# An encoder step in fp32: two accumulators per weight tile, products with high weight parts first

## The chip, the cores and the metric

The kernel runs on one core of a Trainium2 chip. The metric is the device time of one launch in microseconds (us), lower is better; times given are medians over runs of the same program. All inputs and outputs are fp32 and lie in device memory at the start and at the end.

## The reference

One step of a streaming encoder with two layers over 640 token rows (512 of a new prompt, 8 running streams of 16), width 1024. Layer 0 is a convolution module and a gated feed-forward block, then one shared key and value are projected, layer 1 is attention over chunks and a second feed-forward block. What the change touches is layer 0:

```python
def swiglu_ffn(h, g, w_in, w_out):                 # w_in 1024 x 5632, w_out 2816 x 1024
    a, b = jnp.split(rms_norm(h, g) @ w_in, 2, axis=-1)
    return h + (jax.nn.silu(a) * b) @ w_out

def conv_module(h, hist, g, w_pw1, b_pw1, w_dw, b_dw, ln_g, ln_b, w_pw2, b_pw2):
    a, gate = jnp.split(rms_norm(h, g) @ w_pw1 + b_pw1, 2, axis=-1)
    glu = a * jax.nn.sigmoid(gate)
    full = jnp.concatenate([hist.astype(glu.dtype), glu], axis=1)
    y = lax.conv_general_dilated(                  # depthwise, 31 taps, causal
        full, w_dw[:, None, :].astype(full.dtype), window_strides=(1,), padding="VALID",
        dimension_numbers=("NWC", "WIO", "NWC"), feature_group_count=D_MODEL) + b_dw
    y = jax.nn.silu(layer_norm(y, ln_g, ln_b))
    return h + y @ w_pw2 + b_pw2, full[:, -CONV_HIST:]
...
    # run_trunk: layer 0 = conv_module, swiglu_ffn; layer 1 = attention, swiglu_ffn; final rms_norm
```

## The kernel before, in words

Activations are kept transposed, features on the 128 partitions and tokens along the free axis, in two groups: group 0 has 256 columns, group 1 has 384. So a weight tile is the stationary operand of a matmul, and the tokens stream past.

An fp32 product is made of three matmuls in a rounded type. `wsplit` loads a tile of 128 x 2048 weights into `raw` (SP's queue, L139), copies it to the high part `whi` on ScalarE (L150) and takes the low part `wlo` = raw − whi in two pieces (L154): part of the columns on VectorE, and `pool` quarters of them on POOL (three quarters in the feed-forward block of layer 0, two in the second projection). Each of the three tiles has two buffers, so a load must wait until the subtraction of the tile two before it has read `raw`. Activations are split alike (`xsplit`, L159 on ScalarE, L160 on VectorE). `mm3` then runs, for each of the 8 slices along the contraction, the products high·high (L170), low weight·high (L171) and high weight·low (L172) into one accumulator in PSUM. There are four such accumulators (`mmt`, tile name `mm`).

A weight tile of the first projection, and of the feed-forward block's input, feeds two accumulators (`ab`: the value and the gate). `glu` and `ffn_in` fill the first with `mm3`, then the second. `pw2` (second projection of the convolution module) and `ffn_out` also have two outputs per weight tile, one after the other.

The depthwise convolution is shared out by channel block: on VectorE (`conv`, L434 and L437, one operation per tap), on ScalarE and POOL (`conv_pool`, L416 and L417), and on TensorE (`conv_pe`, L469). For the last, `conv_pe_load` stores a block of `gs` or `gp` (the GLU's outputs) to a scratch `sc` in device memory (L452) and reads it back four times with a shift into `x4` (L455, shown as `x<-sc` in the profile); these transfers stand in SP's queue like the weight loads. LayerNorm (`conv_ln`) takes means by summing blocks on POOL (L195) and then over partitions on TensorE (L204); L226 and L230 make the power −1/2, L216 spreads it over the partitions, and L489 multiplies by it.

The string `PLAN` lists the steps of layer 0 (a and b: `glu` of the two groups, l and p: loading and running the convolution on TensorE, q and d: the convolution on POOL and VectorE, n: LayerNorm, w: `pw2`, r: the norm before the feed-forward block, f: one chunk of that block for group 0). This is the order in which the program is written. The final order on each engine is then made by a scheduler ahead of time, from its own estimates and from priorities: what is written under `tc.high_priority` is put forward. So an edit of one helper can move instructions on all engines. On the chip each engine takes its own list strictly in order. A chunk of the feed-forward block is 6 tiles of `ffn_in`, then 4 weight tiles of `ffn_out` whose results VectorE adds to the residual `h` (L303). After the three chunks written in `PLAN` come a shared one and three of group 1.

Attention and the second feed-forward block (L968, L913) use code of their own.

## Time and profile before

| | |
|---|---|
| median of 3 runs | 1549.51 us (1548.63 to 1552.37) |
| profiled execution, its own time | 1551.3 us |
| span of the profile | 1549.5 us |
| mean granted clock of TensorE | 0.984 |
| TensorE matmuls | 10770 recorded, busy 1471.7 us (95%) |
| VectorE busy | 1050.1 us (68%) |
| ScalarE busy | 662.4 us (43%) |
| POOL busy | 443.8 us (29%) |
| moved by DMA | 199.95 MB, mean 129 GB/s |

The span is the time between the first and the last instruction that the profiler saw on the core. "PE" is TensorE's matmul stream and "PEld" its weight loads, which run beside matmuls; DVE is VectorE, ACT ScalarE, POOL GpSimd, and SPq the queue in which SP issues transfers. L numbers are lines of the kernel before. In rows of the timeline the bracket names the idle time ahead of the instruction and what ended it.

### The profile page before, as it was taken

How to read it: one execution, taken by the hardware profiler on the slowest of the kernel's cores; microseconds unless marked ns; L12 is line 12 of the kernel's file. 1: busy time of each engine (PE TensorE's matmuls, PEld its weight loads, DVE VectorE, ACT ScalarE, POOL GpSimd, SP SyncE). 2: the span in 40 equal slices, each digit the busy share in tenths (PEclk: the TensorE clock that was granted, in tenths of full speed). 3: DMA queues.
4: the chain of work that ended last, by engine and by line, in shares of the span. 5: the costliest groups of instructions: out<-in, count | busy, mean ns of one | idle time of the engine just before them, and what ended most of it. 6: DMA issues, size and time to landing. Idle time of an engine off the chain costs nothing.

```text
span 1549.5 us, 26569 instructions
## 1 busy us (share of the span) xinstructions
PE 1471.7 (95%) x10770; PEld 1398.9 (90%) x10770; DVE 1050.1 (68%) x1863; ACT 662.4 (43%) x1173; POOL 443.8 (29%) x403
## 2 busy tenths in 40 slices
PE   5888998989999999999999999999989999999997
PEld 5878888989999999999988798886989999999997
DVE  6994999988555455457576767566796476476455
ACT  4544454535423323235454445443554244244244
POOL 6865568877501000001321211110411121121110
PEclk9999999999999999999999999998999999999998
DMA  7784434444421333433655545453103213213211
GB/s 236 234 228 142 137 113 159 148 157 153 147 82 55 129 116 129 135 118 126 202 183 201 174 140 205 133 175 114 55 28 109 82 56 109 82 55 109 82 55 68
DMA packets 59658, 199.95 MB, mean 129 GB/s; under 512 B 10128, under 2 KB 22672, under 8 KB 46736
## 3 DMA queue, kind: packets, MB, share of 16 engines
q1 hardware_dynamic: 59248, 197.96, 39.1%
q8 instruction: 84, 1.38, 0.4%
q10 hardware_dynamic: 288, 0.31, 0.1%
q14 instruction: 38, 0.31, 0.1%
HBM read 187.02 MB, written 11.22 MB: 128 GB/s over the span
## 4 chain that ended last, share of the span: by engine, by line
PE 71%; DVE 16%; ACT 3%; issue 3%; DMA 3%; POOL 2%; SPq 0%; POOLq 0%; DVEq 0%; ACTq 0%
PE mm L170 12%; PE mm L172 12%; PE mm L171 12%; PE pb L968 6%; DVE w L437 5%; DVE wlo L154 4%; PE pc L968 4%; PE pa L968 4%; PE pb L170 1%; PE pb L171 1%; PE pb L172 1%; PE pa L172 1%; PE pa L170 1%; PE pc L170 1%; PE pc L172 1%
## 5 line engine op out<-in xcount | busy, mean ns | idle before, releaser
L171 PE MATMUL mm<-x,wlo 128*128 128x256 f32 (+1 forms) x1344 | 416.8, 312 | 15.4 <-DVE wlo L154 14.9
L170 PE MATMUL mm<-x,whi 128*128 128x256 f32 (+1 forms) x1344 | 413.3, 312 | 6.4 <-ACT x L159 3.7
L172 PE MATMUL mm<-x,whi 128*128 128x256 f32 (+1 forms) x1344 | 412.7, 311 | 0.5
L150 ACT ACTIVATE whi<-raw 128x2048 fp32r<-128x2048 f32 (+2 forms) x117 | 197.7, 1694 | 232.6 <-PE mm L172 138.8
L171 PEld LDWEIGHTS mm<-x,wlo 128*128 128x128 f32 x1344 | 257.1, 192 | 18.7 <-DVE wlo L154 17.5
L170 PEld LDWEIGHTS mm<-x,whi 128*128 128x128 f32 x1344 | 254.5, 191 | 11.2 <-ACT x L159 4.1
L172 PEld LDWEIGHTS mm<-x,whi 128*128 128x128 f32 x1344 | 255.1, 191 | 2.9 <-DVE x L160 1.8
L154 DVE TENSOR_TENSOR wlo<-raw,whi 128x2048 fp32r<-128x2048 f32 (+5 forms) x117 | 214.0, 1832 | 62.2 <-ACT whi L150 61.2
L154 POOL TENSOR_TENSOR wlo<-raw,whi 128x1536 fp32r<-128x1536 f32 (+3 forms) x50 | 145.7, 2918 | 69.0 <-ACT whi L150 69.0
L913 POOL TENSOR_TENSOR raw<-raw 128x512 f32<-128x512 f32 x38 | 50.5, 1330 | 332.3 <-DVE raw L913 257.5
L171 PE MATMUL mm<-hid,wlo 128*128 128x256 f32 (+1 forms) x352 | 107.7, 308 | 6.6 <-DVE wlo L154 6.6
L172 PE MATMUL mm<-hid,whi 128*128 128x256 f32 (+1 forms) x352 | 105.8, 307 | 0.2
L170 PE MATMUL mm<-hid,whi 128*128 128x256 f32 (+1 forms) x352 | 104.6, 307 | 0.1
L437 DVE SCALAR_TENSOR_TENSOR w<-gp,dwv,w 128x384 f32<-128x384 f32 x180 | 103.9, 612 | 0.8
L195 POOL TENSOR_TENSOR acc<-sq,sq 128x384 f32<-128x384 f32 (+1 forms) x8 | 8.1, 1006 | 258.2 <-ACT sq L179 258.1
L171 PEld LDWEIGHTS mm<-hid,wlo 128*128 128x128 f32 x352 | 66.0, 188 | 7.8 <-DVE wlo L154 7.8
L417 POOL TENSOR_TENSOR y<-y,cvt 128x256 f32<-128x256 f32 (+1 forms) x60 | 69.3, 1154 | 6.3 <-ACT cvt L416 4.0
L172 PEld LDWEIGHTS mm<-hid,whi 128*128 128x128 f32 x352 | 65.7, 188 | 0.6 <-DVE hid L160 0.6
L159 ACT ACTIVATE whi<-raw 128x1024 fp32r<-128x1024 f32 x38 | 39.4, 1054 | 61.6 <-PE pc L172 18.1
L170 PEld LDWEIGHTS mm<-hid,whi 128*128 128x128 f32 x352 | 65.2, 188 | 0.4 <-ACT hid L159 0.3
L968 PE MATMUL pa<-x0f,whi 128*128 128x320 f32 x228 | 61.2, 316 | 2.5 <-DVE t L913 2.3
L195 POOL TENSOR_TENSOR acc<-acc,sq 128x384 f32<-128x384 f32 (+1 forms) x48 | 52.7, 1097 | 28.9 <-ACT sq L179 27.5
(317 smaller groups left out, 3391.4 us busy)
## 6 DMA issues: line engine op xcount, KB each, us to landing
raw<-in_w_in SPq DMA_DIRECT2D x62, 1024.0 KB
raw<-in_w_out SPq DMA_DIRECT2D x36, 768.0 KB
raw<-in_w_pw SPq DMA_DIRECT2D x22, 1024.0 KB
cache<-in_ck SPq DMA_DIRECT2D x32, 512.0 KB
cache<-in_cv SPq DMA_DIRECT2D x32, 512.0 KB
raw<-in_w_kq SPq DMA_DIRECT2D x8, 1024.0 KB
x<-sc SPq DMA_DIRECT2D x16, 368.0 KB
raw<-in_w_out SPq DMA_DIRECT2D x4, 1024.0 KB
```

What stands on the lines that cost most here:

```text
L150: nc.scalar.activation(out=hi[:, a:b], in_=raw[:, a:b], func=AF.Copy)
L154: eng.tensor_tensor(out=lo[:, a:b], in0=raw[:, a:b], in1=hi[:, a:b].bitcast(F32), op=ALU.subtract)
L159: nc.scalar.activation(out=hi, in_=src, func=AF.Copy)
L170: nc.tensor.matmul(ps, wh, xh, start=(i == 0), stop=False)
L171: nc.tensor.matmul(ps, wl, xh, start=False, stop=False)
L172: nc.tensor.matmul(ps, wh, xl, start=False, stop=(i == last))
L195: last["acc"] = eng.tensor_tensor(out=acc[:, :n], in0=prev, in1=s(), op=ALU.add)
L417: nc.gpsimd.tensor_tensor(out=y[g][:, c, :], in0=y[g][:, c, :], in1=pr[:, :n], op=ALU.add)
L437: nc.vector.scalar_tensor_tensor(out=dst, in0=src, scalar=wj, in1=dst, op0=ALU.mult, op1=ALU.add)
L913: ENG[e].tensor_tensor(out=out, in0=a, in1=b, op=op)
L968: nc.tensor.matmul(ps, a[:, c], b[:, k, :], start=(first and k == 0 and i == 0), stop=(k == 3 and i == 2), skip_group_check=not first)
```

## The change

A new helper, `mm3s`, takes a list of accumulators. It first runs, for each accumulator in turn, both products with the high weight part over all slices, and then, again for each in turn, the products with the low weight part. `ffn_in`, `glu` and `pw2` take their two accumulators from the pool at once and hand both to `mm3s`; `out_tile` becomes `out_tiles`, which does the same for two neighbouring outputs of `ffn_out`. The number of matmuls, their shapes and operands stay. `mm3` stays in use for the projections of attention. In the changed file the lines after the helper stand 9 later at first, then 3 to 7 (L204 becomes L213, L303 L310, L437 L441, L452 L456, L455 L459, L469 L473, L489 L493).

```diff
+    def mm3s(pss, wtss, xs):
+        for ps, wts in zip(pss, wtss):
+            for i, ((wh, wl), (xh, xl)) in enumerate(zip(wts, xs)):
+                nc.tensor.matmul(ps, wh, xh, start=(i == 0), stop=False)
+                nc.tensor.matmul(ps, wh, xl, start=False, stop=False)
+        for ps, wts in zip(pss, wtss):
+            for i, ((wh, wl), (xh, xl)) in enumerate(zip(wts, xs)):
+                nc.tensor.matmul(ps, wl, xh, start=False, stop=(i == len(wts) - 1))
+
...
         wh, wl = wsplit(wsrc[j], 16, P, pool=pool)
         for g in groups:
             n = GR[g][1]
-            ps = []
-            for ab in range(2):
-                pt = mmt()
-                mm3(pt[:, :n], [(wh[:, (ab * 8 + k) * P:(ab * 8 + k + 1) * P],
-                                 wl[:, (ab * 8 + k) * P:(ab * 8 + k + 1) * P]) for k in range(KT)],
-                    xk(xs[g], range(KT)))
-                ps.append(pt[:, :n])
+            ps = [mmt()[:, :n] for _ in range(2)]
+            mm3s(ps, [[(wh[:, (ab * 8 + k) * P:(ab * 8 + k + 1) * P],
+                        wl[:, (ab * 8 + k) * P:(ab * 8 + k + 1) * P]) for k in range(KT)]
+                      for ab in range(2)], xk(xs[g], range(KT)))
...
-    def out_tile(wts, ch, b, m, g, hid):
+    def out_tiles(wts, ch, bs, ms, g, hid):
         wh, wl = wts
         n = GR[g][1]
-        pt = mmt()
-        mm3(pt[:, :n], [(wh[:, (b + k) * P:(b + k + 1) * P], wl[:, (b + k) * P:(b + k + 1) * P])
-                        for k in range(ch)], xk(hid[g], range(ch)))
-        with tc.high_priority(offset=HP):
-            nc.vector.tensor_tensor(out=hp(g, m), in0=pt[:, :n], in1=hp(g, m), op=ALU.add)
+        ps = [mmt()[:, :n] for _ in ms]
+        mm3s(ps, [[(wh[:, (b + k) * P:(b + k + 1) * P], wl[:, (b + k) * P:(b + k + 1) * P])
+                   for k in range(ch)] for b in bs], xk(hid[g], range(ch)))
+        for m, pt in zip(ms, ps):
+            with tc.high_priority(offset=HP):
+                nc.vector.tensor_tensor(out=hp(g, m), in0=pt, in1=hp(g, m), op=ALU.add)
...
-            for m in range(m0, m0 + mg):
-                for g in groups:
-                    out_tile(ws[-1], ch, (m - m0) * ch, m, g, hid)
+            for g in groups:
+                out_tiles(ws[-1], ch, range(0, mg * ch, ch), range(m0, m0 + mg), g, hid)
```

`glu` and `pw2` are edited as `ffn_in` is.

What the scheduler makes of it is seen in the lists of the engines. First TensorE at the first weight tile of the third feed-forward chunk of group 0 (`whi_457`, `wlo_458`; mm_459 and mm_460 are the two accumulators). Before:

```order
L172 MATMUL mm_454_3601<-hid_392_3054,whi_451_3575 128x256
L170 MATMUL mm_459_3629<-x_256_2033,whi_457_3623 128x256
L170 MATMUL mm_460_3654<-x_256_2033,whi_457_3623 128x256
L171 MATMUL mm_459_3629<-x_256_2033,wlo_458_3624 128x256
L172 MATMUL mm_459_3629<-x_256_2033,whi_457_3623 128x256
L170 MATMUL mm_459_3629<-x_256_2033,whi_457_3623 128x256
L171 MATMUL mm_459_3629<-x_256_2033,wlo_458_3624 128x256
```

And now the end of the same tile, behind 32 high products:

```order
L177 MATMUL mm_460_3630<-x_256_2033,whi_457_3623 128x256
L178 MATMUL mm_460_3630<-x_256_2033,whi_457_3623 128x256
L181 MATMUL mm_459_3629<-x_256_2033,wlo_458_3624 128x256 x8
L181 MATMUL mm_460_3630<-x_256_2033,wlo_458_3624 128x256 x8
L177 MATMUL mm_466_3692<-x_256_2033,whi_464_3686 128x256
```

The low part stood third in the tile, and now it stands thirty-third; the next tile follows directly in both.

Second, SP's queue during the convolution module. `raw` tiles are weight loads, `sc` the stores to the scratch, `x4` the shifted reads, `out_convs` the output of the convolution state. Before:

```order
L139 DMA raw_130_1158<-in_w_pw1 128x2048
L541 DMA out_convs<-gs_96 1024x1x368
L452 DMA sc_124_1108<-gs_96 128x740
L452 DMA sc_128_1151<-gs_96 128x740
L139 DMA raw_192_1444<-in_w_pw1 128x2048
L455 DMA x4_125_1110<-sc_124_1108 32x4x736 x4
L139 DMA raw_199_1506<-in_w_pw1 128x2048
L455 DMA x4_129_1153<-sc_128_1151 32x4x736 x4
```

And now:

```order
L139 DMA raw_130_1158<-in_w_pw1 128x2048
L139 DMA raw_192_1444<-in_w_pw1 128x2048
L545 DMA out_convs<-gs_96 1024x1x368
L456 DMA sc_124_1108<-gs_96 128x740
L456 DMA sc_128_1151<-gs_96 128x740
L139 DMA raw_199_1506<-in_w_pw1 128x2048
L459 DMA x4_125_1110<-sc_124_1108 32x4x736 x4
L139 DMA raw_206_1567<-in_w_pw1 128x2048
```

Two weight loads (raw_192, raw_199) have moved ahead of the stores and of the first shifted read. Likewise raw_116 now stands ahead of sc_97, and raw_222 ahead of sc_215.

Third, POOL at the LayerNorm of group 0, where `acc` sums the squares, `rst2` is the power, and wlo_219 and wlo_224 are low halves of the second projection's weights. Before:

```order
L195 TENSOR_TENSOR acc_173_1373<-acc_173_1373,sq_177_1383 128x256
L154 TENSOR_TENSOR wlo_219_1704<-raw_217_1702,whi_218_1703 128x1024
L195 TENSOR_TENSOR acc_173_1373<-acc_173_1373,sq_178_1386 128x256
L195 TENSOR_TENSOR acc_173_1373<-acc_173_1373,sq_179_1389 128x256
L195 TENSOR_TENSOR acc_173_1373<-acc_173_1373,sq_180_1392 128x256
L230 TENSOR_TENSOR rst2_182_1399<-rst_181_1397,mhalf_82 128x2
L154 TENSOR_TENSOR wlo_224_1763<-raw_222_1761,whi_223_1762 128x1024
```

And now:

```order
L204 TENSOR_TENSOR acc_173_1373<-acc_173_1373,sq_179_1389 128x256
L204 TENSOR_TENSOR acc_173_1373<-acc_173_1373,sq_180_1392 128x256
L154 TENSOR_TENSOR wlo_224_1763<-raw_222_1761,whi_223_1762 128x1024
L239 TENSOR_TENSOR rst2_182_1399<-rst_181_1397,mhalf_82 128x2
L154 TENSOR_TENSOR wlo_229_1822<-raw_227_1820,whi_228_1821 128x1024
```

The half wlo_224 has moved from behind the power to the place ahead of it. On ScalarE its high part (whi_223) now stands ahead of the last square (sq_180), and on VectorE its other half stands ahead of the multiplications of L489. On VectorE five depthwise operations fewer (172 instead of 177) lie between these multiplications and the subtraction of wlo_458, two of them earlier and three later; and the subtraction of wlo_118, which frees the buffer that raw_192 waits for, stands ahead of the last GLU product of group 0 and no longer behind it.

More of the change, by code (lines that the diff above doesn't have):

```diff
@@ L312, in ffn_out @@
                 continue
-            for m in range(m0, m0 + mg):
-                for g in groups:
-                    out_tile(ws[-1], ch, (m - m0) * ch, m, g, hid)
+            for g in groups:
+                out_tiles(ws[-1], ch, range(0, mg * ch, ch), range(m0, m0 + mg), g, hid)
         if mg == 4:
             for g in groups:
-                for m in range(KT):
-                    out_tile(ws[m // mg], ch, (m % mg) * ch, m, g, hid)
+                for m in range(0, KT, 2):
+                    out_tiles(ws[m // mg], ch, ((m % mg) * ch, (m % mg + 1) * ch), (m, m + 1), g,
+                              hid)
     def ffn(pool, w_in, w_out, xs, groups, chunks, pl=0, og=None, cm=CM, pad=(0, 0)):
@@ L499, in pw2 @@
             wh, wl = wsplit(w_pw2[m2], 16, P, pool=PL2[g])
-            for i in range(2):
-                m = 2 * m2 + i
-                pt = mmt()
-                mm3(pt[:, :n], [(wh[:, (i * 8 + k) * P:(i * 8 + k + 1) * P],
-                                 wl[:, (i * 8 + k) * P:(i * 8 + k + 1) * P]) for k in range(KT)],
-                    xk(z, range(KT)))
-                nc.vector.scalar_tensor_tensor(out=hp(g, m), in0=pt[:, :n], scalar=col(V_BPW2, m),
+            ps = [mmt()[:, :n] for _ in range(2)]
+            mm3s(ps, [[(wh[:, (i * 8 + k) * P:(i * 8 + k + 1) * P],
+                        wl[:, (i * 8 + k) * P:(i * 8 + k + 1) * P]) for k in range(KT)]
+                      for i in range(2)], xk(z, range(KT)))
+            for i, pt in enumerate(ps):
+                m = 2 * m2 + i
+                nc.vector.scalar_tensor_tensor(out=hp(g, m), in0=pt, scalar=col(V_BPW2, m),
                                                in1=hp(g, m), op0=ALU.add, op1=ALU.add)
```

11 lines of the change are left out of this document (4 added, 7 removed).

## Prediction

> **What bounds the kernel now.** I read the page's busy shares first. TensorE is busy for nearly the whole span, so a change that only reorders its matmuls can earn no more than the idle time that it removes.
> ```profile
> PE 1471.7 (95%) x10770; PEld 1398.9 (90%) x10770; DVE 1050.1 (68%) x1863; ACT 662.4 (43%) x1173; POOL 443.8 (29%) x403
> ```
> Then the view of waits, for TensorE in the first 400 us, where most of the edited code runs (columns: total us, times, longest).
> ```profile
> PE mm L171 <- DVE wlo L154: 21.6, 18, 3.6
> ...
> PE mm L469 <- DMA x<-sc: 10.5, 2, 5.4
> ...
> PE w L216 <- POOL rst L230: 2.5, 2, 1.4
> ```
> The edit is aimed at the first line: the matmul with the low weight part (L171) is the second of every three, so it stands at the front as soon as a new weight tile begins, and it waited 18 times for VectorE's subtraction. 21.6 us, 1.4% of the run, is the whole direct wait. Whether it can be had depends on what VectorE does meanwhile, so I cut the stretch into windows (start:end and length, then busy us of each engine, granted clock, DMA share, GB/s).
> ```profile
> core 0: us, PE busy (x) PEld busy (x) DVE busy (x) ACT busy (x) POOL busy (x), PEclk, DMA share, GB/s
> 200.00:240.00 40.00, 36.22 (x281) 35.24 (x280) 40.00 (x66) 23.38 (x35) 29.97 (x15) 0.96 0.36 105
> ...
> 280.00:320.00 40.00, 35.62 (x296) 34.16 (x295) 39.97 (x69) 20.69 (x28) 35.51 (x20) 1.00 0.46 145
> 320.00:340.00 20.00, 16.03 (x125) 15.63 (x124) 14.99 (x20) 7.67 (x8) 14.69 (x9) 0.91 0.53 185
> 340.00:420.00 80.00, 77.03 (x565) 75.52 (x564) 59.11 (x67) 39.47 (x53) 55.09 (x26) 1.00 0.44 146
> 420.00:720.00 300.00, 300.00 (x1839) 300.00 (x1838) 151.48 (x193) 97.49 (x120) 10.89 (x13) 1.00 0.33 109
> ```
> There are three regimes. From about 160 to 325 us VectorE has no free time (40.00 of 40) and TensorE idles a tenth of it: VectorE is the bound. From 340 TensorE is nearly full, and from 420 to 720 it is full (300.00 of 300): nothing the edit does to waits can pay there. After 720 come attention and the second feed-forward block, which the edit does not touch. So the run's end is VectorE's end at about 325, plus what TensorE still has to do after it. Most of the 18 waits lie in the VectorE-bound stretch, where a matmul that waits less merely meets the next wait. The handover at its end is the place that counts, seen in the timeline (start, us, engine and operation; in brackets the idle time before).
> ```profile
> 323.66 1.92 ACT L150 ACTIVATE whi<-raw 128x2048 fp32r<-128x2048 f32 x1 [7.02 <-DMA raw<-in_w_in]
> ...
> 325.63 0.50 PE L170 MATMUL mm<-x,whi 128*128 128x256 f32 x2 [0.41 <-ACT whi L150]
> ...
> 325.85 3.79 DVE L154 TENSOR_TENSOR wlo<-raw,whi 128x512 fp32r<-128x512 f32 x1
> ...
> 329.69 0.58 PE L171 MATMUL mm<-x,wlo 128*128 128x256 f32 x1 [3.56 <-DVE wlo L154]
> ...
> 332.84 0.41 PE L170 MATMUL mm<-x,whi 128*128 128x256 f32 x1
> 333.06 0.31 PE L171 MATMUL mm<-x,wlo 128*128 128x256 f32 x1
> ```
> This is the first weight tile of the third feed-forward chunk. TensorE runs two high matmuls, the first of either accumulator, then idles 3.56 us until the low part ends, and then runs at half pace to 333.06.
>
> **The change, part by part.** It adds and removes no matmul, load, copy or transfer. What it moves:
>
> (a) *The low products go last.* A pair of accumulators now takes 32 high products before the first low one, where it took two here. In a steady stretch these are the first and the last of 28 matmuls with 256 columns:
> ```profile
> 299.76 0.28 PE L171 MATMUL mm<-x,wlo 128*128 128x256 f32 x1
> ...
> 302.83 0.28 PE L171 MATMUL mm<-x,wlo 128*128 128x256 f32 x1
> ```
> They start 3.07 / 27 = 0.114 us apart, and 30 × 0.114 = 3.4 us of work fits in front of the wait at 329.69, which is 3.56 long: I take −3.4. The bounds are −3.56 (all of the wait) and 0 (the weights' high part itself comes late, as the 0.41 at 325.63 hints).
>
> (b) *The half pace behind that wait.* From the start at 329.69 to that at 333.06 there are 15 steps in 3.37 us, where 15 × 0.114 = 1.7 would do: 1.7 are lost. Without a gap of over 3 us I expect no such stretch: −1.7, bounds −1.7 and 0. The Trainium skill, "TensorE: Matmul & The Clock Gate", "What's actually happening", says the clock falls to half after an idle window of about 3.4 us and comes back after as long a busy one; the 3.56 us gap and the 3.37 us behind it agree.
>
> (c) *The waits after 340.* Two are left in the stretch where TensorE is the bound, and both are shorter than the 3.4 us of cover:
> ```profile
> 357.39 0.38 PE L171 MATMUL mm<-x,wlo 128*128 128x256 f32 x1 [1.74 <-DVE wlo L154]
> 384.20 0.38 PE L171 MATMUL mm<-hid,wlo 128*128 128x256 f32 x1 [0.95 <-DVE wlo L154]
> ```
> 1.74 + 0.95: −2.7, bounds −2.7 and 0. Nothing is late next: 420 to 720 is full already.
>
> (d) *VectorE's list.* Ahead of the low part waited for at 329.69, counted from the multiplications by the LayerNorm scale (L489) on, five depthwise operations (L437) fewer stand in the list, and one low half (wlo_224) that stood between those multiplications now stands ahead of them.
> ```profile
> L437 DVE SCALAR_TENSOR_TENSOR w<-gp,dwv,w 128x384 f32<-128x384 f32 x180 | 103.9, 612 | 0.8
> ...
> 116.00:155.00 39.00, 34.26 (x243) 32.20 (x242) 18.65 (x33) 18.11 (x27) 19.78 (x17) 0.96 0.46 143
> ...
> 149.83 1.05 POOL L230 TENSOR_TENSOR rst<-rst,mhalf 128x2 f32<-128x2 f32 x1 [0.94 <-DVE rst L226]
> ...
> 151.59 2.35 POOL L154 TENSOR_TENSOR wlo<-raw,whi 128x1024 fp32r<-128x1024 f32 x1 [0.72 <-ACT whi L150]
> ...
> 154.00 1.22 DVE L154 TENSOR_TENSOR wlo<-raw,whi 128x1024 fp32r<-128x1024 f32 x1
> ```
> Two of the five and the low half are now done before the LayerNorm, where VectorE was busy only 18.65 of 39 us, so its idle time hides them; three are put off past 329.69, where VectorE has slack (14.99 of 20, then 59.11 of 80). Operations in a row start 0.53 to 0.61 apart: 5 × 0.53 + 1.22 = 3.9. I take −3.9 on VectorE's end; bounds −4.3 (at 612 ns) and 0 (if VectorE has to wait for TensorE's sums somewhere in the stretch).
>
> (e) *The queue on SP.* The scheduler has moved weight loads ahead of the transfers that shift the convolution's input, and a load whose buffer isn't free holds all that is queued behind it. Timeline of SP's queue, VectorE's row that frees the buffer, and the chain that ended last:
> ```profile
> 82.87 1.42 SPq L452 DMA_DIRECT2D sc<-gs  x2
> 86.08 0.33 SPq L139 DMA_DIRECT2D raw<-in_w_pw  x1
> 91.74 1.74 SPq L455 DMA_DIRECT2D x<-sc  x4
> 95.34 0.35 SPq L139 DMA_DIRECT2D raw<-in_w_pw  x1
> ...
> 83.31 2.74 DVE L154 TENSOR_TENSOR wlo<-raw,whi 128x2048 fp32r<-128x2048 f32 x1
> ...
> 82.87 8.81 DMA sc<-gs
> ...
> 93.05 10.56 DMA x<-sc
> ...
> 103.81 5.62 PE mm L469 x63
> ```
> The load at 86.08 waited for the subtraction that ends at 86.05. It now stands ahead of the `sc` stores that went out at 82.87: 86.05 − 82.87 = 3.2 us later at the least if nothing else moves, and its 1 MB (1.05 million bytes) shares the transfers' way; the load at 95.34 stands ahead of `x<-sc` too. The window from 80 to 116 carried 229 GB/s:
> ```profile
> 80.00:116.00 36.00, 30.57 (x251) 25.81 (x250) 34.95 (x70) 16.16 (x26) 23.48 (x22) 0.91 0.83 229
> ```
> 1.05 MB at 229 GB/s is 4.6 us, but before, it ran beside `sc` as well, so most of it isn't new. The chain goes through `sc`, `x<-sc`, L469 and on to the LayerNorm of the first group, so a delay here is a delay there. Bounds 0 (the subtraction comes earlier, since it is moved ahead of VectorE's last GLU product) and 3.2 + 4.6 = 7.8; I take +4.0, near the wait that has a row.
>
> (f) *POOL and ScalarE before the first LayerNorm's power.* TensorE waits for that power (2.5 us in the view of waits, two times). The 2.35 us subtraction of wlo_224 stood behind the power (149.83) and now stands ahead of it. Bounds 0 (POOL does it while it waits for squares) and 2.35. Its high part is now ahead of the last square on ScalarE, so it will be ready just when POOL should go on: +2.0.
>
> (g) *The handover to attention.* The last two evictions of group 1 were
> ```profile
> 729.37 0.54 DVE L303 TENSOR_TENSOR h<-mm,h 128x384 f32<-128x384 f32 x1
> ...
> 732.64 0.55 DVE L303 TENSOR_TENSOR h<-mm,h 128x384 f32<-128x384 f32 x1
> ```
> 3.3 us apart, 18 matmuls. As a pair the first is complete only 6 matmuls ahead of the second, so it comes 12/18 × 3.3 = 2.2 us later; the second's time stays. The squares and the sum of the first must then run inside about 1 us. Bounds 0 and 2.2; most of it is covered by the wait for the second: +0.5.
>
> **The sum.** VectorE's end: (e) +4.0, (f) +2.0, (d) −3.9 = +2.1. TensorE behind it: (a) −3.4, (b) −1.7, (c) −2.7, (g) +0.5 = −7.3. Together −5.2 us. The profiled execution took 1551.3 us (its span 1549.5 and 1.8 around it), 1.8 above the median of 1549.5; the change is taken off the median: 1544.3. About 0.3%, 4.6 us, is what a measurement of this kernel can tell from no change; the border of "faster" is then 1544.9, so this forecast lies close to it.
>
> **Rivals.** *The latency was the bound, not VectorE's load.* If the full VectorE windows were loops of waiting (VectorE waits for TensorE's sums, TensorE for its low parts), 3.4 us of cover, which at least nearly reaches the longest of the 18 waits, would take away all 21.6, plus 1.7 of half pace, less (e), (f) and (g): 21.6 + 1.7 − 6.5 = 16.8, so 1532.7. Against it: VectorE has hardly any idle time at 200 to 320 to be such a loop. 0.11.
>
> *Slower: the loads block SP's queue in every round.* Before each of the convolution's four rounds on TensorE one weight load has moved ahead of a store or a shift. If each round lost 4.0, as I charge one, the delay would be 16.0 and the total −5.2 + 12.0 = +6.8: 1556.3. For it: both waits for `x<-sc`, 10.5 us, are already on the chain. Against it: the two other rounds did not wait. It decides from a delay of 4.0 + 5.2 = 9.2 on, and shows as slower from 14. 0.21.
>
> *Nothing is gained at the handover.* The cover moves the wait from the first tile of the third chunk to the next, since VectorE and POOL still have to make every low part and the transfers at 320 to 340 are no earlier: (a), (b) and (c) vanish, (d), (e), (f), (g) leave +2.6: 1552.1. For it: ScalarE sat 7.02 us until the raw weights landed at 323.66, so a transfer stands in the same place. 0.20.
>
> *Shared stationary operands are loaded once.* Each high weight part now serves two matmuls in a row, (wh,xh) and (wh,xl). In this kernel L739 and L740 already use the same stationary tile one after the other, and each of them loads it, 64 times:
> ```profile
> L740 PEld LDWEIGHTS w<-KL,QQ 128*128 128x128 f32 x64 | 12.1, 189 | 0.7
> L739 PEld LDWEIGHTS w<-KK,QQ 128*128 128x128 f32 x64 | 12.0, 188 | 3.8 <-issue 2.9
> ```
> By these rows nothing is saved, and the loads run beside the matmuls anyway. If a third of the edited loads vanished and each freed 10 ns of the 114 that a matmul takes, some 1500 of them would give −15 beyond the sum, near 1529. 0.03. The Trainium skill, "TensorE: Matmul & The Clock Gate", "Step-by-step: what each phase is for", says a stationary operand can be loaded once and used by many matmuls; the rows of L739 and L740 show no such saving.
>
> **How the numbers follow.** The forecast, VectorE-bound with a gain behind the handover, has 0.45. Its own range is 1538 (with (e) and (f) at nothing) to 1551 (with (e) at 7.8 and (c) lost). The range over all cases must take in the slower rival near 1556 and the latency rival at 1532.7: 1532 to 1556 leaves about 2 in 10 out. Faster: 0.29 of the forecast's 0.45 + 0.11 + 0.03 = 0.43. Slower: 0.15 of that rival's 0.21 + 0.05 of the third's = 0.20. Same: the rest, 0.37.
>
> **What would show it.** Right: waits of the low products on `wlo` far below 21.6 us, yet VectorE still full from 200 to 320; no idle time of over 1 us and no half pace at the third chunk's first tile; the window 340:420 close to 80 busy; 420:720 unchanged in length. For (e): the third run of the shifted-input matmuls (before at 103.81) some 4 us later; for (f): the power (before at 149.83) about 6 later. Wrong: VectorE with idle time at 200 to 320 and a much earlier end (the latency rival); the shifted-input matmuls over 9 us later (the slower one); or a new wait for `whi` or a raw transfer where the low part was waited for (the third).

## The result, and the profile after

The changed kernel takes 1566.95 us (median of 5 runs, 1558.54 to 1572.46), the kernel before, run beside it, 1551.27 (1548.63 to 1552.37). The ratio is 1.010, with a 95% interval of 1.0069 to 1.0131: slower by some 15 us, where 5 us less was forecast. The profiled execution of after took 1565.2 us and its span is 1563.4, 13.9 more than the span before. The first line of its page:
```profile
PE 1477.5 (95%) x10770; PEld 1405.4 (90%) x10770; DVE 1058.5 (68%) x1863; ACT 665.1 (43%) x1173; POOL 438.3 (28%) x403
```
Beside the line of before, TensorE is busy 5.8 us longer with the same 10770 matmuls, and idle 85.9 us (1563.4 − 1477.5) for 77.8, 8.1 longer. So the loss is in part waiting and in part slower pace: the granted clock of the two profiles is 0.980 for 0.984.

The view of waits of after, TensorE in the first 440 us (total us, times, longest):
```profile
PE mm L473 <- DMA x<-sc: 13.6, 2, 8.7
...
PE mm L178 <- DVE x L160: 5.7, 6, 1.8
PE mm L177 <- ACT whi L150: 5.0, 5, 2.1
...
PE w L225 <- POOL rst L239: 3.9, 2, 2.7
...
PE w L225 <- DVE mst L484: 3.0, 1, 3.0
...
PE mm L181 <- DVE wlo L154: 1.1, 4, 0.4
```
The waits that the edit was aimed at are gone: 1.1 us on `wlo` where there were 21.6. In their place stand a longer wait for the convolution's shifted input (`x<-sc`, 13.6 for 10.5) and waits for activations (`x`), high parts, the LayerNorm's power (`rst`) and, new, its mean (`mst`). The windows of after (columns as in the prediction's):
```profile
200.00:240.00 40.00, 35.23 (x254) 34.04 (x255) 39.72 (x65) 21.38 (x36) 22.43 (x13) 0.96 0.35 106
280.00:320.00 40.00, 34.59 (x277) 33.57 (x276) 40.00 (x59) 19.51 (x28) 33.02 (x16) 0.96 0.47 160
...
320.00:340.00 20.00, 16.53 (x125) 16.13 (x124) 19.93 (x34) 6.85 (x8) 13.32 (x9) 0.91 0.45 152
340.00:420.00 80.00, 74.53 (x555) 73.11 (x554) 57.81 (x72) 41.05 (x53) 52.84 (x24) 0.96 0.42 146
...
440.00:720.00 280.00, 280.00 (x1704) 280.00 (x1703) 139.85 (x181) 90.56 (x106) 8.41 (x10) 1.00 0.32 109
```
The three regimes are as before, and VectorE is as full from 200 to 320; but it stays full some 15 us longer (19.93 of 20 from 320 to 340, where it had 14.99), and TensorE does less beside it (35.23 of 40 where it did 36.22, 34.59 where it did 35.62). The tile that the forecast was about, in the timeline of TensorE:
```profile
342.85 0.28 PE L178 MATMUL mm<-x,whi 128*128 128x256 f32 x1
343.35 2.15 PE L181 MATMUL mm<-x,wlo 128*128 128x256 f32 x16 [0.23 <-DVE wlo L154]
345.34 0.28 PE L177 MATMUL mm<-x,whi 128*128 128x256 f32 x1
```
Here the edit does what it says: a gap of 0.23 us for one of 3.56, and 16 low products in 2.0 us, at full pace. But the low part ends 13.7 us later than before (339.72 + 3.57 = 343.29 instead of 325.85 + 3.79 = 329.64).

The delay shows at three places, and each is a norm. First the LayerNorm of group 0, POOL's timeline before and then after:
```profile
143.12 3.44 POOL L154 TENSOR_TENSOR wlo<-raw,whi 128x1024 fp32r<-128x1024 f32 x1 [1.18 <-ACT whi L150]
146.52 2.37 POOL L195 TENSOR_TENSOR acc<-acc,sq 128x256 f32<-128x256 f32 x3
149.83 1.05 POOL L230 TENSOR_TENSOR rst<-rst,mhalf 128x2 f32<-128x2 f32 x1 [0.94 <-DVE rst L226]
```
```profile
143.17 0.74 POOL L204 TENSOR_TENSOR acc<-sq,sq 128x256 f32<-128x256 f32 x1 [10.83 <-ACT sq L188]
143.87 3.47 POOL L154 TENSOR_TENSOR wlo<-raw,whi 128x1024 fp32r<-128x1024 f32 x1
147.30 4.31 POOL L204 TENSOR_TENSOR acc<-acc,sq 128x256 f32<-128x256 f32 x5
152.68 1.45 POOL L204 TENSOR_TENSOR acc<-acc,sq 128x256 f32<-128x256 f32 x1 [1.07 <-ACT sq L188]
154.09 2.71 POOL L154 TENSOR_TENSOR wlo<-raw,whi 128x1024 fp32r<-128x1024 f32 x1
156.76 0.70 POOL L239 TENSOR_TENSOR rst<-rst,mhalf 128x2 f32<-128x2 f32 x1
```
Before, one low half stood among the sums of the squares, and the power followed the last sum; after, two stand between the first sum and the power, which comes 6.9 us later. Not all of this is the norm's own: the fourth run of the convolution on TensorE, ahead of it, starts at 121.84 for 118.68, 3.2 later. From that start to the power it is 34.9 us for 31.1, so these lists cost 3.8. Next the norm ahead of the feed-forward block, on VectorE, the last split of its normalized activations, before and after:
```profile
206.42 0.75 DVE L160 TENSOR_TENSOR x<-n,x 128x256 fp32r<-128x256 f32 x2
```
```profile
219.39 1.91 DVE L160 TENSOR_TENSOR x<-n,x 128x256 fp32r<-128x256 f32 x2
```
That is 207.2 against 221.3, 14.1 us: a weight subtraction and a GLU product now stand ahead of it in VectorE's list. TensorE feels it only in part. Last the LayerNorm of group 1, its power on POOL, before and after:
```profile
374.10 0.86 POOL L230 TENSOR_TENSOR rst<-rst,mhalf 128x3 f32<-128x3 f32 x1 [0.43 <-DVE rst L226]
```
```profile
390.69 0.86 POOL L239 TENSOR_TENSOR rst<-rst,mhalf 128x3 f32<-128x3 f32 x1 [0.57 <-DVE rst L235]
```
16.6 us later, of which 13.9 are left at the end.

The pattern is alike in all three: splits of the next weights stand ahead of a norm's squares, sums or splits, on engines that take their lists strictly in order. But the sizes differ. At the third norm the chain itself took no longer, 23.1 us from the first sum of squares (367.64) to the power for 22.6 (from 351.50); one more weight tile stands ahead of that first sum, and 13.7 of the 16.6 us were there already at the chunk's first tile. The scheduler made these lists from its own estimates, which no trace shows. One thing that the edit changes for it is that a high part's buffer comes free 16 low products (1.8 us at 0.114 each) sooner; the product held back, below, says whether that is enough of a reason.

### The profile page after: what moved, and what is told of

Its sections match the earlier page's. It is cut to its first block, busy times and chain, and to the rows that moved or that the text cites. A ratio compares the mean times of both kernels' runs of the same rounds, so it can differ in the third digit from the quotient of the medians.

```text
span 1563.4 us, 26604 instructions
## 1 busy us (share of the span) xinstructions
PE 1477.5 (95%) x10770; PEld 1405.4 (90%) x10770; DVE 1058.5 (68%) x1863; ACT 665.1 (43%) x1173; POOL 438.3 (28%) x403
## 4 chain that ended last, share of the span: by engine, by line
PE 69%; DVE 15%; issue 2%; ACT 2%; DMA 2%; POOL 0%; DVEq 0%; POOLq 0%; ACTq 0%; SPq 0%
PE mm L178 8%; PE mm L177 8%; PE mm L181 8%; PE pb L972 6%; DVE w L441 5%; PE mm L170 4%; PE mm L171 4%; PE mm L172 4%; PE pc L972 4%; DVE wlo L154 4%; PE pa L972 4%; PE pb L170 1%; PE pb L171 1%; PE pb L172 1%; PE pa L172 1%
## 5 line engine op out<-in xcount | busy, mean ns | idle before, releaser
L177 PE MATMUL mm<-x,whi 128*128 128x256 f32 (+1 forms) x1088 | 311.6, 314 | 9.7 <-ACT whi L150 5.0
L178 PE MATMUL mm<-x,whi 128*128 128x384 f32 (+1 forms) x1088 | 310.7, 312 | 5.7 <-DVE x L160 5.7
L154 DVE TENSOR_TENSOR wlo<-raw,whi 128x2048 fp32r<-128x2048 f32 (+5 forms) x117 | 225.4, 1929 | 53.9 <-ACT whi L150 31.4
L177 PEld LDWEIGHTS mm<-x,whi 128*128 128x128 f32 x1088 | 206.4, 193 | 14.1 <-ACT whi L150 6.0
L178 PEld LDWEIGHTS mm<-x,whi 128*128 128x128 f32 x1088 | 206.1, 192 | 7.5 <-DVE x L160 7.5
L181 PE MATMUL mm<-x,wlo 128*128 128x384 f32 (+1 forms) x1088 | 171.8, 310 | 1.2 <-DVE wlo L154 1.1
L181 PEld LDWEIGHTS mm<-x,wlo 128*128 128x128 f32 x1088 | 162.4, 190 | 2.2 <-DVE wlo L154 2.2
L177 PE MATMUL mm<-hid,whi 128*128 128x256 f32 (+1 forms) x352 | 102.1, 317 | 5.1 <-ACT hid L159 3.0
L178 PE MATMUL mm<-hid,whi 128*128 128x256 f32 (+1 forms) x352 | 103.0, 316 | 3.4 <-DVE hid L160 3.4
L441 DVE SCALAR_TENSOR_TENSOR w<-gp,dwv,w 128x384 f32<-128x384 f32 x180 | 104.2, 612 | 1.1
L170 PE MATMUL mm<-x,whi 128*128 128x256 f32 (+1 forms) x256 | 80.5, 314 | 0.7 <-DVE h L310 0.7
L171 PE MATMUL mm<-x,wlo 128*128 128x256 f32 (+1 forms) x256 | 79.9, 312 | 0.0
L172 PE MATMUL mm<-x,whi 128*128 128x256 f32 (+1 forms) x256 | 79.5, 310 | 0.0
L204 POOL TENSOR_TENSOR acc<-sq,sq 128x384 f32<-128x384 f32 (+1 forms) x8 | 8.6, 1076 | 250.2 <-ACT sq L188 250.2
L177 PEld LDWEIGHTS mm<-hid,whi 128*128 128x128 f32 x352 | 68.1, 196 | 5.7 <-ACT hid L159 3.4
L178 PEld LDWEIGHTS mm<-hid,whi 128*128 128x128 f32 x352 | 68.2, 195 | 4.0 <-DVE hid L160 3.8
L159 ACT ACTIVATE hid<-t 128x256 fp32r<-128x256 f32 (+1 forms) x44 | 20.7, 471 | 113.0 <-DVE t L299 70.2
```

The source lines that it names most:

```text
L154: eng.tensor_tensor(out=lo[:, a:b], in0=raw[:, a:b], in1=hi[:, a:b].bitcast(F32), op=ALU.subtract)
L159: nc.scalar.activation(out=hi, in_=src, func=AF.Copy)
L170: nc.tensor.matmul(ps, wh, xh, start=(i == 0), stop=False)
L171: nc.tensor.matmul(ps, wl, xh, start=False, stop=False)
L172: nc.tensor.matmul(ps, wh, xl, start=False, stop=(i == last))
L177: nc.tensor.matmul(ps, wh, xh, start=(i == 0), stop=False)
```

## The experiments

Every ratio is to runs of the kernel before made together with the experiment, with its 95% interval; differences in us are those of the two medians.

### Which part costs

**Only the feed-forward block**: `mm3s` in `ffn_in` and `ffn_out`; `glu` and `pw2` as before.

> The helper is used in ffn_in and ffn_out alone; glu and pw2 are as before, and SP's queue in the convolution module has its old order. Theory A (the loss comes from the lists of the convolution module): the LayerNorm's power of group 0 at 149.8 as before, total -6 to +1 us against before. Rival B (the loss comes from the feed-forward stretch itself, where VectorE's subtractions now run beside POOL's and take longer): power at 149.8 as before, but the depthwise work on VectorE ends 6 to 10 us later, total +5 to +9.

1552.42 against 1549.97: 1.0009 (0.9994 to 1.0024). The whole of the edit in the part where most of the 21.6 us stood gains nothing in sum. Its view of waits:
```profile
PE mm L177 <- DVE t L294: 9.7, 6, 3.7
...
PE mm L171 <- DVE wlo L154: 2.5, 2, 1.8
...
PE mm L181 <- DVE wlo L154: 0.7, 3, 0.2
```
The wait for `wlo` fell to 3.2 us: 2.5 in `glu` and `pw2`, which run as before, and 0.7 in the edited block. A wait for VectorE's product that reads a finished accumulator (`t`, 9.7 us) took its place: VectorE was the bound, as the prediction had it against the latency rival. The third chunk alone gains 3.6 us (below, with POOL's list held at the last norm), so the rest of the block loses several us here; this run shows only the sum.

**Only `glu`**: the first projection alone uses `mm3s`.

> The helper is used in glu alone; pw2 and the feed-forward block are as before. SP's queue has the order of the changed kernel. Theory A: third run of the shifted-input matmuls 2 to 4 us later than 103.8, the power near 156.5 instead of 149.8, total +6 to +15. Rival B: the power as late, but the end only 0 to +5, because the feed-forward stretch takes it up.

1559.96 against 1549.97: 1.0066 (1.0042 to 1.0089), +10.0. Its power at the first LayerNorm:
```profile
156.81 0.71 POOL L239 TENSOR_TENSOR rst<-rst,mhalf 128x2 f32<-128x2 f32 x1
```
That is as late as in after (156.76), so the first norm's delay comes from `glu`.

**Only `pw2`**, in a later group of runs:

> The helper in pw2 alone. Theory E: +4 to +7 against before. Rival F: -1 to +2.

1556.52 against 1550.8: 1.0042 (1.0025 to 1.0059), +5.7. The three parts alone cost 10.0, 2.4 and 5.7, 18 together, where the whole costs some 15. The place is the norm behind `pw2`; window of `pw2` alone, then of before:
```profile
210.00:220.00 10.00, 6.27 (x33) 6.08 (x32) 10.00 (x15) 3.89 (x6) 4.73 (x3) 0.68 0.43 76
```
```profile
210.00:220.00 10.00, 7.88 (x56) 7.69 (x55) 10.00 (x13) 4.54 (x8) 9.84 (x6) 0.83 0.56 124
```
33 matmuls where there were 56, and a granted clock of 0.68 for 0.83.

**The changed kernel again**, unedited:

> The changed kernel once more, beside the others on the same chip. +10 to +18 by both theories; its single times spread over 1558 to 1572, more than those of before (1548 to 1552), and that spread should show again.

1564.96 (1558.26 to 1570.41) against 1549.97: 1.0091 (1.0065 to 1.0117). The span of its profile is 1556.4. There the third run of the convolution on TensorE started at 104.38 and the power at 153.88, 0.6 and 4.1 later than before; in after it was 2.5 and 6.9. In the nine profiles of kernels whose `glu` is as before, the third run starts anywhere from 101.79 to 105.08, so one profile can't price a delay of 2 us there. What repeats is the way from the fourth run to the power: 34.9 us in both profiles of after and with `glu` alone, 31.1 in before. So of after's 6.9, the part that comes with the transfers varies between executions, and 3.8 are there each time. At the first low part of the third chunk this profile is 6.0 us late (335.66 for 329.64), and 6.9 at the end.

### Is it SP's queue?

**One high product held back.** It stands behind the low ones, so that the high part's buffer comes free at the tile's end, and SP's queue has its old order:

```diff
-                nc.tensor.matmul(ps, wh, xl, start=False, stop=False)
+                if ps is not pss[-1] or i < len(wts) - 1:
+                    nc.tensor.matmul(ps, wh, xl, start=False, stop=False)
...
+        nc.tensor.matmul(pss[-1], wts[-1][0], xs[-1][1], start=False, stop=True)
```

> As the changed kernel, but one product of 32 with the high weight part is held back to the very end of the pair, so that the high part's buffer comes free when the tile ends, as before. SP's queue then has its old order (raw_192 behind sc_124 and sc_128). Theory A: the early release of the high part is what moves the weight loads ahead; power at 149 to 152, total -6 to +3. Rival B: the lists of SP don't matter, total like the changed kernel, +10 to +18.

1569.3 against 1549.97: 1.012 (1.0098 to 1.0143), +19, no better than after. Its runs of the convolution on TensorE, and then POOL's timeline at the first norm:
```profile
103.20 5.79 PE L476 MATMUL mm<-x,w 128*32 128x256 f32 x64 [7.31 <-ACT whi L150]
...
118.31 3.66 PE L476 MATMUL mm<-x,w 128*32 128x256 f32 x64 [0.74 <-ACT t L387]
```
```profile
151.79 3.38 POOL L154 TENSOR_TENSOR wlo<-raw,whi 128x1024 fp32r<-128x1024 f32 x1 [1.19 <-ACT whi L150]
155.13 1.52 POOL L207 TENSOR_TENSOR acc<-acc,sq 128x256 f32<-128x256 f32 x2
157.99 0.71 POOL L242 TENSOR_TENSOR rst<-rst,mhalf 128x2 f32<-128x2 f32 x1 [1.35 <-DVE rst L238]
```
Before, the runs started at 103.81 and 118.68, so both are on time here, and yet the power comes at 157.99, 8.2 late: SP's order is not the cause. The second low half of `pw2` again stands ahead of the last sums, though the high part's buffer comes free no sooner than before. So the earlier release alone isn't what moves the lists; which of the scheduler's estimates does is open.

**First norm's lists and SP's queue as before**, with the changed matmuls; **first norm's lists alone**. The edit puts the high parts' copies behind the squares, and POOL's low halves behind the sums and the power, where they stood before:

```diff
+            aft = ((sq[4], accs[3]), (sq[7], pw), None, None)[m2] if g == 0 else None
...
+                with tc.issue_after(aft[0].ins) if aft else ExitStack():
                     nc.scalar.activation(out=hi[:, a:b], in_=raw[:, a:b], func=AF.Copy)
```

> The changed kernel, with the lists of ScalarE and POOL at the LayerNorm of group 0 put back to the order of before (copies whi_218 and whi_223 behind the fifth and the last square, subtractions wlo_219 and wlo_224 behind the fourth sum and behind the power). SP's queue stays as changed. Theory A (delays at the LayerNorm are carried to the end): power 3 us earlier than in the changed kernel, at 151 to 154, end 3 us earlier too, +9 to +12 against before. Rival B (the feed-forward stretch sets the end whatever comes ahead of it): power as early, end unchanged, +13 to +17.

> As the last one, and the weight loads in SP's queue also put back behind the convolution's stores and shifted reads. Theory A: power at 149 to 151.5 as before; what is left is the longer subtractions on VectorE in the feed-forward stretch, so +3 to +8 against before. If the LayerNorm's delay were all: 0 to +3. Rival B: +12 or more.

Lists alone: 1564.35 against 1549.37, 1.0105 (1.009 to 1.0121). With SP's queue too: 1565.88, 1.0102 (1.0085 to 1.012). The first norm is mended (power at 151.77 and 152.17, for 156.76; 31.7 us behind the fourth run in both), and nothing is gained. Where the gain went is seen in the power of the LayerNorm of group 1, in the two kernels:
```profile
385.80 0.86 POOL L243 TENSOR_TENSOR rst<-rst,mhalf 128x3 f32<-128x3 f32 x1 [0.22 <-DVE rst L239]
```
```profile
392.97 0.86 POOL L244 TENSOR_TENSOR rst<-rst,mhalf 128x3 f32<-128x3 f32 x1
```
11.7 and 18.9 later than before. The first low part of the third chunk ends only 3.3 and 5.9 late (332.97 and 335.51), so 8.4 and 13.0 us are lost between it and this power, where after lost 2.9 (16.6 − 13.7). What was won at the first norm is lost by the last: two and three weight tiles slid ahead of the last norm's sums, where in after it is one. One norm at a time can't be judged in this kernel.

**The first norm even earlier, in the kernel before**: POOL's halves of the first two `pw2` tiles behind the power.

> The kernel before, with the first two weight tiles of the second projection split only behind the last square and the power, so that nothing stands between the statistics of group 0. Theory A (VectorE's stretch starts with the LayerNorm and is carried to the end): power 2 to 4 us earlier than 149.8, total -4 to -1. Rival B: power as early, but the end unchanged, since the split then comes late for TensorE: -1 to +3.

1551.71 against 1549.37: 1.0018 (1.0007 to 1.0029). The power came 1.9 earlier (147.96) and the time did not fall. But the fourth run of the convolution, which stands ahead of the edit, started 1.0 earlier too (117.69 for 118.68), so the lists themselves gained 0.9. That is too little to tell what an earlier first norm is worth.

### The norms, one by one

**Only `glu`, first norm's lists as before:**

> The helper in glu alone, and the lists of ScalarE and POOL at the LayerNorm of group 0 put back to the order of before. Theory C (the early release of the high part lets the scheduler put splits ahead of the LayerNorm's statistics; delays there are carried to the end): power at 150.5 to 153 instead of 156.8, total +2 to +5 against before instead of +10. Rival D (glu costs elsewhere, in the first norm or the convolution's rounds): total stays at +8 to +11.

1554.4 against 1550.1: 1.0023 (1.0009 to 1.0037), power at 151.66. With `glu` alone 1.0066, so more than half of `glu`'s cost is the first norm's order; the intervals lie apart.

**The full change, lists of both LayerNorms as before**; and **only the feed-forward block, list of the second as before**:

```diff
+        return {16: (sq[1], accs[0]), 17: (sq[3], accs[2]), 18: (sq[5], accs[4]),
+                19: (sq[7], accs[6]), 20: (sq[7], pw)}[i]
```

> The changed kernel with the lists of ScalarE and POOL put back at both LayerNorms: at group 0 as in the run before, and at group 1 the splits of the last five weight tiles of the third chunk again behind the squares, sums and power that they stood behind. Theory C: with both gates back, 0 to +5 against before. Rival B (the subtractions that run beside POOL's hold VectorE, and so the depthwise work and the second LayerNorm): depthwise work ends 8 us later than before, power of group 1 as much later, total +7 to +12.

> The helper in the feed-forward block alone, and the lists at the LayerNorm of group 1 put back. Theory C: power of group 1 at 373 to 376, total -3 to 0 against before. Rival: the list of the second LayerNorm has slack there, total unchanged, +1 to +3.

The full change: 1561.59, 1.0067 (1.0045 to 1.0088), +11.5 against medians and about 10.4 by the ratio, where the first list alone had left 1.0105. The feed-forward block: 1549.88, 0.999 (0.9973 to 1.0006) for 1.0009; the power at 374.09 is on time (374.10 before), but the gain is within the intervals.

**The full change, both LayerNorms, `pw2` as before:**

> As the run with both LayerNorms' lists put back (the helper everywhere, +10 measured), but pw2 as before. The helper in glu alone with its list put back gave +4, in the feed-forward block alone 0. Theory E (the parts add up, and pw2 makes the rest): +3 to +5 against before. Rival F (glu's and the feed-forward block's changes together move VectorE's subtractions into POOL's): +7 to +11.

1555.64 against 1550.8: 1.003 (1.0014 to 1.0046), +4.8. Taking `pw2` out of the full change with both LayerNorms gives 0.37% back, 5.7 us, just what `pw2` alone costs; the two intervals touch.

**Only `pw2`, with VectorE's list at the norm ahead of the feed-forward block as before**; and **the full change with all three norms as before**:

```diff
+        return ((None, pw, None), (None, None, xlo))[j]
...
+                with tc.issue_after(marks["r", 0][1].ins) if c == 6 else ExitStack():
                     nc.vector.scalar_tensor_tensor(out=gp[:, c, HIST:HIST + 384], in0=t[:, :n], scalar=1.0,
```

> The helper in pw2 alone (+6.5 measured), and VectorE's list at the norm ahead of the feed-forward block put back: the subtraction of the second feed-forward tile and a GLU product again behind the last split of the normalized inputs. Theory G (the same early split, at a third norm): last split of these inputs ends near 208 instead of 215.7 us, total 0 to +3 against before. Rival H (pw2's pairs themselves are late, since both outputs now end with the tile): total stays at +5 to +8.

> The changed kernel with the lists put back at all three norms (both LayerNorms and the norm ahead of the feed-forward block). Theory G: +2 to +6 against before, where two of the three gave +10. Rival H: +8 to +11.

The two disagree. With `pw2` alone: 1556.13 against 1550.06, 1.0043 (1.0028 to 1.0058), no gain over 1.0042; that norm's power itself came about 3 us later than in `pw2` alone (1.8 of it already at the fourth run of the convolution), and the last split ended no earlier (215.6 for 215.7), so the restored list was no clean test. In the full change: 1555.81, 1.003 (1.0018 to 1.0043), where two norms had left 1.0067 (1.0045 to 1.0088): a gain of about 5.7 us, the intervals just apart. So the three norms' lists carry 9 or 10 of the full change's 15 us. The remaining 5.8 is the size of what `pw2` costs alone, but what costs it was not settled. The profile of this kernel (1558.42 us) points to the pace of TensorE: its span is 7.1 above before's, the power of group 1 stands at 375.17, only 1.1 late, TensorE idles 0.8 more than before (78.6) and is busy 6.3 longer (1478.0). A matmul that waited, and a window behind it:
```profile
339.35 0.38 PE L183 MATMUL mm<-x,whi 128*128 128x256 f32 x1 [1.91 <-ACT whi L153]
```
```profile
340.00:350.00 10.00, 10.00 (x53) 10.00 (x52) 7.65 (x6) 1.68 (x2) 8.18 (x3) 0.54 0.37 117
```
Before has 89 matmuls and a clock of 1.00 in the same window. At 0.54 some 4.6 of the 10 us are lost (an estimate from the clock), in this one execution.

### Is it VectorE's load?

**All of the low parts of the first chunks on POOL**, in the changed kernel (`PFA = 3` to `PFA = 4`): VectorE loses its 128 x 512 subtractions.

> The changed kernel with all four quarters of the low weight part on POOL in the three feed-forward chunks beside the convolution (three before), so that VectorE makes none there. Theory A (VectorE is the bound from 160 to 340 and its subtractions are stretched by POOL's): the depthwise work on VectorE ends 15 to 25 us earlier than in the changed kernel, total -8 to -16 against it, so -2 to +8 against before. Rival B: POOL, busy 32 of 40 us, becomes the bound and TensorE waits for its low parts: 0 to +10 against the changed kernel.

1584.76 against 1549.37: 1.0228 (1.021 to 1.0245). VectorE's last depthwise operation came 18.4 us earlier than before, at 312.7, and the kernel is slower by 35 us: POOL is now the bound, and the last norm stands in its list. The waits of TensorE from 340 to 470 us:
```profile
PE w L213 <- POOL acc L204: 11.2, 2, 10.8
```
The power of that norm comes at 407.87, 33.8 late. Here the run's end does not hang on VectorE's end of the depthwise work, as the prediction's sum assumed, but on the LayerNorm of group 1 behind it.

### What the cover is worth by itself

**Only the third chunk of group 0**, its six tiles of `ffn_in` and its `ffn_out`, with POOL's list at the last norm as before; all else is the kernel before. Run twice:

```diff
+def HIF(j, g):
+    return g == 0 and 12 <= j < 18
...
+            if HIF(j, g):
+                ps = [mmt()[:, :n] for _ in range(2)]
+                mm3s(ps, wts, xk(xs[g], range(KT)))
```

> The helper only in the third feed-forward chunk of group 0, where TensorE becomes the bound, with POOL's list as before: nothing but TensorE's order changes there. It prices the terms of the prediction for the tail by themselves: -3.4 for the wait at the first tile, -1.7 for the half pace behind it, -2.7 for the two later waits. As predicted: -5 to -8. Rival (the second LayerNorm, which follows VectorE's depthwise work, stands on the path and takes the place of those waits): -2 to +2.

> The helper in the third chunk alone once more, beside the last one on the same chip: -2 to -6 against before.

1546.55 against 1550.1, 0.9973 (0.9958 to 0.9987), and 1547.09 against 1550.8, 0.9977 (0.996 to 0.9994): faster by 3.6 us, between the two expected ranges. No earlier stage's order moves here, so this is the gain of (a), (b) and (c) without the losses ahead of them. The window over the tile and the view of waits of TensorE from 320 to 440 us:
```profile
320.00:340.00 20.00, 19.30 (x167) 18.97 (x167) 12.52 (x20) 9.93 (x10) 16.66 (x9) 1.00 0.47 161
```
```profile
PE w L237 <- DVE mst L545: 2.7, 1, 2.7
PE mm L183 <- DVE x L171: 1.2, 1, 1.2
PE mm L188 <- ACT whi L159: 0.7, 1, 0.7
PE mm L182 <- DVE wlo L165: 0.2, 1, 0.2
```
TensorE is busy for 19.30 of 20 us where it had 16.03, at a clock of 1.00 for 0.91. But 2.7 + 1.2 + 0.7 = 4.6 us of other waits stand behind it, on the LayerNorm of group 1 above all; 0.4 of them, on `whi`, stood in before too. 7.8 were expected, 7.8 − 4.2 = 3.6, and 3.6 were measured; that it fits to a tenth is chance, as the interval reaches some 2 us either way. The Trainium skill, "TensorE: Matmul & The Clock Gate", "What's actually happening", ties the half clock to an idle window of about 3.4 us; that the half pace went with the 3.56 us gap agrees, though the last section has a shorter gap that did the same.

**The same, with that norm's means ahead of a weight subtraction and a split on VectorE:**

> The helper in the third chunk alone (-4 measured), and on VectorE the means of the second LayerNorm put ahead of one hidden tile's split and one weight subtraction again, where they stood before. TensorE waited 2.7 us for these means. If that wait is on the path: -1 to -3 more, -5 to -7 against before; if it only hides the next wait: -3 to -5.

1545.28 against 1550.8: 0.9967 (0.9953 to 0.998), 5.5 us faster, the best version tried. Its interval overlaps that of the kernel without this step, beside which it ran, so the step's own 1.8 us is not shown.

## Why the prediction was wrong

What bounds the kernel was read rightly: VectorE is full to the end of its stretch, the feed-forward block's direct waits bring nothing in sum, and nothing moves from 440 to 720. The latency rival fell with the first experiment, and the rival of shared stationary operands with the page: 10770 weight loads for 10770 matmuls, as before. That nothing is gained at the handover isn't borne out either, since the third chunk alone gains. Wrong was the sum.

- **(a), (b), (c), −7.8.** The mechanism was right at the place (0.23 us for 3.56, no half pace, `wlo` waits gone). By itself it is worth 3.6. The step "nothing is late next: 420 to 720 is full already" failed: the second LayerNorm's mean was late next. In after TensorE waits 3.0 us for it too, and the delay is as large at the end (13.9) as at the tile (13.7; 6.9 and 6.0 in the second profile), so nothing of the 7.8 arrived. The premise of (b), that half pace needs a gap of over 3 us, did not hold either (last section).
- **(d), −3.9.** The term that failed most. From the first norm's power to the low part at 343.29 the delay grew from 6.9 to 13.7, so VectorE took 6.7 us more where 3.9 less were forecast; in the second profile it grew from 4.1 to 6.0, 2.0 more. The depthwise operations cost what they did (612 ns each). The counted list was right, but it left out that the norm ahead of the feed-forward block was pushed back, and that the subtractions take longer: the 18 in a row ahead of that low part sum to 36.4 us, and 34.5 in the second profile, for 27.8 before (the last section says how).
- **(e), +4.0, and (f), +2.0.** The third run of the convolution came 2.5 later in after and 0.6 in the second profile, and with `glu` as before it moves by 3.3 between profiles: the size of (e) is not shown, but 4.0 was too large for both. From the fourth run to the power it is 3.8 more, so (f) was too small. Their sum, 6.0 for 6.9, is about right for after, by luck. And it can't be taken as the loss: mending (f) alone gave nothing back.
- **(g), +0.5.** Harmless. The last two evictions stand at 747.95 and 748.67, 0.7 apart for 3.3, as worked out; the delay at the second is 16.0 and at the end 13.9, so no time was lost there.
- **The slower rival** had the sign and a price of +6.8, and the wrong mechanism: with SP's old order the kernel was no faster, in two ways. Of the two, the place to look was POOL's and ScalarE's lists at every norm, and not only at the first, where (f) had one row of the same kind.

The step behind all of these: the change was costed at the places of the lists that looked critical, and the sum took the rest of the order as unchanged. But the lists had moved at every norm.

## What to carry to other kernels

When an edit regroups the work of one engine, and a scheduler orders the lists of all ahead of time, look at every short dependent chain (a norm's squares, sums and power) in the new lists, and compare what stands ahead of its last link; the direct waits that vanish tell little. Make such a change only where its wait is the last one to end, here one chunk of many, and pin the order of the chains around it. When a wait goes, ask which row ends next in the same place: here it took back half of the gain.

## What the hardware showed

How long a subtraction of 128 x 512 on VectorE takes, 0.96 to 3.22 us in these rows, depends on what POOL does. POOL's and VectorE's subtractions in the timelines of after:
```profile
280.42 3.51 POOL L154 TENSOR_TENSOR wlo<-raw,whi 128x1536 fp32r<-128x1536 f32 x1 [0.64 <-ACT whi L150]
288.71 3.48 POOL L154 TENSOR_TENSOR wlo<-raw,whi 128x1536 fp32r<-128x1536 f32 x1 [2.27 <-ACT whi L150]
293.57 3.51 POOL L154 TENSOR_TENSOR wlo<-raw,whi 128x1536 fp32r<-128x1536 f32 x1
```
```profile
281.26 3.22 DVE L154 TENSOR_TENSOR wlo<-raw,whi 128x512 fp32r<-128x512 f32 x1
289.79 2.96 DVE L154 TENSOR_TENSOR wlo<-raw,whi 128x512 fp32r<-128x512 f32 x1
296.67 0.96 DVE L154 TENSOR_TENSOR wlo<-raw,whi 128x512 fp32r<-128x512 f32 x1
```
POOL's end at 283.93, 292.19 and 297.08; VectorE's end at 284.48, 292.75 and 297.63, each 0.55 us later, however early they began. Over the 20 subtractions of this stretch, the duration less the time in which a POOL subtraction ran is 0.55 us in the median, in before, after and three of the other kernels alike; what differs is the overlap, 1.09 us each in before, 1.45 in after and 1.08 in the third-chunk kernel. So a subtraction of VectorE makes no progress while POOL subtracts, and "busy" on VectorE holds such waiting; the depthwise operations kept their 612 ns. The Trainium skill, "SBUF — State Buffer", "Who interferes with whom", states a lock on the shared read port for two-input operations of VectorE against POOL's reads; these rows agree. Over the 18 ahead of the low part the overlap sums to 17.1 us in before and 26.1 in after: 9.0 more, which covers the 8.6 that VectorE's subtractions took longer. What sets it off is open: with `glu` alone it is 17.2, with all three norms' lists as before still 24.1, and no kernel changed the overlap alone.

The half pace also came without a gap of 3 us. In after TensorE waited 2.41 us (from 315.44 to 317.85), worked for 2.7, and waited again, with these rows in the timeline and these windows (start:end and length, busy us, then the granted clock) behind it:
```profile
317.85 0.38 PE L178 MATMUL mm<-hid,whi 128*128 128x256 f32 x1 [2.41 <-DVE hid L160]
...
322.61 0.38 PE L177 MATMUL mm<-hid,whi 128*128 128x256 f32 x1 [2.10 <-DVE t L294]
```
```profile
323.00:327.00 4.00, 4.00 (x23) 4.00 (x23) 4.00 (x9) 1.58 (x3) 1.73 (x2) 0.57 0.49 186
327.00:331.00 4.00, 4.00 (x36) 4.00 (x36) 4.00 (x6) 1.91 (x2) 3.16 (x2) 1.00 0.01 4
```
23 matmuls in 4 us where the next 4 us take 36, at a clock of 0.57: new waits of 2 us, near each other, cost half pace just as the one that was removed. By this count 13 matmuls, 1.5 us, are lost there. In the kernel with all three norms' lists as before, ten us at 0.54 of the clock stood behind a wait of 1.91 us.
